# A hybrid four-branch trunk on one Trainium2 core: branch outputs through the weight ring, keys and values of the window branch in its own stage, z gates among the first SSD convolutions

## The chip, the cores and the metric

The kernel runs on one core of one Trainium2 chip. The metric is the device time of one execution in microseconds (us). The engines are called PE (TensorE, the matmuls), DVE (VectorE), ACT (ScalarE), POOL (GpSimd) and SP (SyncE, which here only issues DMAs). Each has its own queue and executes it in order; engines wait for each other through semaphores.

## The reference

One layer, a sequence of 512 tokens, model width 2048, everything in float32. A single combined projection of the normalized input feeds four token mixers of width 1024 and four merge gates:

```python
h = rms_norm(x, norm_w[l])
proj = jnp.einsum("bsd,dn->bsn", h, w_in[l])
(aq, ak, av, ag, bq, bk, bv, bg, cxbc, cdt, cz, dglu, dg, mg) = jnp.split(proj, _split_points(), axis=-1)
ya = diff_attention(aq, ak, av, lam, lam_init, subln_w, bias_a) * silu(ag)   # A: 8 heads, causal
yb = sliding_window_attention(bq, bk, bv, sinks, bias_b) * silu(bg)          # B: window 128, 16 q / 4 kv heads
yc = ssd_mixer(cxbc, cdt, cz, ...)                                           # C: Mamba-2 SSD, gated by silu(cz)
yd = conformer_conv(dglu, ...) * silu(dg)                                    # D: GLU, conv of 31 taps, LayerNorm
up = jnp.einsum("bsir,ird->bsid", branches, w_branch[l])
merged = jnp.sum(jax.nn.sigmoid(mg) * up, axis=2)
x = rms_norm(x + jnp.einsum("bsd,de->bse", merged, w_out[l]), final_norm_w)
```

(The calls are shortened.) `ssd_mixer` first runs a convolution of 4 taps and a SiLU over its x, B and C channels, then works in chunks of 128 tokens with decay matrices from `dt`.

## The kernel before

**Precision.** Each float32 matmul is done as three products of split operands: `x = hi + lo` with both halves in the fast fp32 format, and `hi*hi + lo*hi + hi*lo` summed in PSUM. So each weight piece goes three steps: a DMA into a `wr` tile, an ACT cast to `wh`, a DVE subtraction to `wl` (L289, L296, L297). The hidden state's halves are `hh` and `hl`.

**The weight ring.** `wr`, `wh` and `wl` have three buffers each in pool `wp`. `build_sequence` writes down the order of all weight pieces of the program; `next_piece` hands out the next one and makes pieces up to PLA = 6 ahead, but not beyond `state["limit"]`. SP issues all of these loads.

**Projections.** `proj(c)` is 128 output columns over all 512 tokens: 16 steps of the contraction by three products, 48 products of 512 columns (L410 to L412), into one of three PSUM banks `acc`. The result is multiplied by `rb` (the token norm) on DVE. `silu_of` is two DVE steps around an ACT sigmoid (L604 to L606).

**Stages in time.**
- 0 to about 785 us: the merge gates and one value projection, in groups; their results go to DRAM (`gate_d`).
- to about 1060: SSD (branch C). For each of two groups: convolutions `conv4` of B, C and four x tiles (L693 to L700, four taps on DVE at L697), for the first group the dt chain, then chunk by chunk the decay matrices `se` (L761 to L772 on DVE, ACT and POOL) and their matmuls (L778, L781), then the z gates and the output.
- to about 1440: the conformer convolution (31 taps on DVE, L835), then its LayerNorm and activation to about 1482.
- to about 1711: differential attention (branch A), head by head: queries and keys (L933 to L948), scores (L952, L953), softmax, transposes (L1005), outputs (L1009).
- to about 1873: window attention (branch B) with the same kinds of steps (scores at L952 too, L1069 to L1100).
- to about 2200: the merge. For each branch, `load_y` brings its output back from `y_d` as `yraw` and splits it (L1115, L166, L167) into `yh` and `yl`; four blocks of columns follow, each with four w_branch pieces of 24 products (L482 to L484), a multiplication by the gate tile `gt` and a sum. The pools `yq` of `yh` and `yl` take the space in which `hh` and `hl` lay.
- then the output projection and the final norm, to 2424.

Branch outputs go to `y_d`; some SiLU gates and branch B's keys and values, projected right behind SSD, go to DRAM (`silu_d`, `kv_d`) and come back later. POOL issues those DMAs.

**Order.** The program is written stage by stage, but a scheduler (`TCKW = {"schedule_with_timeline_sim": True}`) sets each engine's order, so work of neighbouring stages is mixed. The weight sequence and the pools bound what it can move.

Of the kernel before, what the change touches and what calls it, by code (L numbers as in the profile page):

```python
# [11 lines left out]
F32 = mybir.dt.float32  # L12
F32R = mybir.dt.float32r
AF = mybir.ActivationFunctionType
ALU = mybir.AluOpType
# [36 lines left out]
def build_sequence():  # L52
    seq = []

    def proj(col):
        for half in range(2):
            seq.append(("p", col, half))

    for half in range(2):
        for col in (CB, CC):  # L60
            seq.append(("p", col, half))
    for r in range(2):
        for kp in range(KH // 2):
            seq.append(("s0", r, kp))
    for col in EARLY[2:]:
        proj(col)
    for gi in range(NGROUP):
        for k in range(KH):
            seq.append(("s1", gi, k))
        for r in rest(gi):  # L70
            for kp in range(KH // 2):
                seq.append(("s2", gi, r, kp))
    for g in range(2):
        for j in range(4):
            if CX + (g * 4 + j) * P not in EARLY:
                proj(CX + (g * 4 + j) * P)
        for j in range(4):
            proj(CZ + (g * 4 + j) * P)
    for j in range(2):
        proj(BK + j * P)  # L80
        proj(BV + j * P)
    for c in range(NB):
        proj(DV + c * P)
        proj(DGT + c * P)
        proj(DG + c * P)
        proj(AG + c * P)
    for j in range(4):
        proj(BG + j * P)
    for h in range(8):
        proj(AQ + h * P)  # L90
        proj(AK + h * P)
    for j in range(8):
        proj(BQ + j * P)
        if j >= 4:
            proj(BG + j * P)
    for br in BRANCHES:
        for nb in range(4):
            for k2 in range(NB // 2):
                seq.append(("u", br, nb, k2))
    for eb in range(3):  # L100
        for k2 in range(KT // 2):
            seq.append(("o", eb * S, k2 * 2, 2, S))
    for eh in range(2):
        for k4 in range(KT // 4):
            seq.append(("o", 3 * S + eh * 256, k4 * 4, 4, 256))
    return seq
# [3 lines left out]
def hybrid_trunk(ctx, tc, x, norm_w, w_in, diff_lambda, diff_subln_w, swa_sinks, ssd_conv_w,  # L110
# [88 lines left out]
    pieces = {}  # L199
    first_s = next(i for i, key in enumerate(seq) if key[0] == "s1")  # L200
    first_late = len(seq) - KT // 4
    state = {"made": 0, "used": 0, "limit": first_s}
# [222 lines left out]
    raw_d = dram.tile([len(EARLY), P, S], F32, name="raw_d")  # L425
    kv_d = dram.tile([4, P, S], F32, name="kv_d")
    silu_d = dram.tile([3, NB, P, S], F32, name="silu_d")
# [10 lines left out]
    mge = open_pool("mge", 3, "right")  # L438
    state["limit"] = first_late
    sums = {}  # L440
# [262 lines left out]
    dtw = load_dt()  # L703
    for g in range(2):
        bT, cT = hold(), hold()
        conv4(CB + g * P, 8 + g, bT)
        conv4(CC + g * P, 10 + g, cT)
        xT = []
        for j in range(4):
            xj = keep("yh")  # L710
            conv4(CX + (g * 4 + j) * P, g * 4 + j, xj)
            xT.append(xj)
# [24 lines left out]
        for t in range(NT - 1):  # L737
# [10 lines left out]
            prev[t + 1] = pv  # L748
        sz = []
        for j in range(4):  # L750
            z = keep("yl")
            silu_of(proj(CZ + (g * 4 + j) * P), z)
            sz.append(z)
        for t in range(NT):
# [51 lines left out]


    for j in range(2):
        for i, c0 in enumerate((BK, BV)):
            kv = hold()  # L810
            V.tensor_tensor(kv, proj(c0 + j * P), rb, op=ALU.mult)
            G.dma_start(kv_d[2 * j + i], kv)
    vtoks = []
# [15 lines left out]
    def conv_taps(c, pad, y):  # L829
# [10 lines left out]
        return [lambda j=j: tap(j) for j in range(31)]  # L840

    def stored_silu(i, c, w):
        sg = hold()
        silu_of(proj(w + c * P), sg)
        G.dma_start(silu_d[i, c], sg)

# [39 lines left out]
    A.copy(rbs, rd)  # L886
    for j in range(4):
        stored_silu(2, j, BG)
# [140 lines left out]
    for j in range(2):  # L1029
        kk, kl = [yp.tile([P, S], F32R, tag="yh", name="kk") for _ in range(2)], [hold(F32R), hold(F32R)]  # L1030
        k = early()
        G.dma_start(k, kv_d[2 * j])
        keys(k, kk, kl)
        kd += [(kk[m], kl[m]) for m in range(2)]
        vT = early()
        G.dma_start(vT, kv_d[2 * j + 1])
        pt = tr_tile()
# [68 lines left out]
    gp = open_pool("gp", 2, "right")  # L1106
    rp = open_pool("rp", 2, "right")
    up = open_pool("up", 4, "right")
    sets = [[acc_tile, acc_tile, acc_tile, lambda: s_tile(0)], [lambda: s_tile(1), tr_tile, tr_tile, o_tile]]

    def load_y(bi):
        his, los = [], []
        for q in range(2):
            raw = rp.tile([P, 4, S], F32, tag="raw", name="yraw")
            G.dma_start(raw, y_d[BRANCHES[bi], 4 * q:4 * q + 4].rearrange("k p s -> p k s"))  # L1115
            hi = yq[bi % 2].tile([P, 4, S], F32R, tag="y", name="yh")
            lo = yq[2 + bi % 2].tile([P, 4, S], F32R, tag="y", name="yl")
            split(raw, hi, lo)
            his.append(hi)
            los.append(lo)  # L1120
        return his, los
# [13 lines left out]

    ys = load_y(0)
    for bi, br in enumerate(BRANCHES):
        for nb in range(4):
# [23 lines left out]
        if bi < 3:  # L1162
            ys = ys_next
    close_pool("up", "rp", "gp", "mp")
    lastp = open_pool("lastp", 4)
# [119 lines left out]
```

## Time and profile before

| | |
|---|---|
| median of 3 runs | 2423.55 us (2423.54 to 2424.19) |
| profiled execution | 2425.63 us, span 2423.9 us |
| mean granted clock of PE | 0.990 |
| PE, DVE, ACT, POOL busy | 98%, 66%, 38%, 15% of the span |

The span runs from the first to the last instruction of the profiled execution; the rest of its own time lies around it. "Busy" counts an engine's instructions, not its waits. The granted clock is the share of full speed that PE was given; its levels are 1.2 and 2.4 GHz, so 0.5 is the lower one throughout a stretch. A window's row gives for each engine the busy time in that stretch.

### The profile page before, as it was taken

The numbers are of one execution on the slowest core, as the hardware profiler recorded it, in microseconds if no ns is written. First come the engines' busy times: TensorE is split into PE (matmuls) and PEld (weight loads), VectorE is DVE, ScalarE is ACT, GpSimd is POOL, SyncE is SP. The second block draws the span as 40 slices with busy tenths as digits, with TensorE's granted clock in tenths as the row PEclk, the third lists the DMA queues.
The fourth block names the chain that finished last, engine by engine and source line by source line (L and its number), as shares of the span: only waits on it lengthen the run. The fifth ranks groups of instructions, "written<-read, shape, count | busy, mean of one in ns | idle before, by whom it ended". The sixth has DMA issues, their size and how long they took to land.

```text
span 2423.9 us, 29417 instructions
## 1 busy us (share of the span) xinstructions
PE 2367.8 (98%) x11141; PEld 1949.8 (80%) x11141; DVE 1597.2 (66%) x2550; ACT 931.6 (38%) x1434; POOL 368.4 (15%) x428
## 2 busy tenths in 40 slices
PE   8989999999999999999999999999998999999998
PEld 7868888888887877888888888888776788888888
DVE  6697877777776678558887887766666444334323
ACT  5344444444544344222222235555465222122222
POOL 1000000000001023110101034222101012233101
PEclk9999999999999999999999999999899999999999
DMA  8554555555556444344343355333232744443423
GB/s 255 148 165 153 171 174 156 163 165 165 165 167 185 115 124 117 108 140 111 106 118 105 109 153 174 102 99 105 74 92 87 257 166 147 148 148 119 150 98 111
DMA packets 299115, 340.22 MB, mean 140 GB/s; under 512 B 14862, under 2 KB 203659, under 8 KB 298974
## 3 DMA queue, kind: packets, MB, share of 16 engines
q1 hardware_dynamic: 267742, 247.84, 34.7%
q0 software_dynamic: 27744, 84.21, 10.3%
q10 hardware_dynamic: 3488, 6.30, 0.8%
q8 instruction: 87, 1.43, 0.2%
q14 instruction: 54, 0.44, 0.1%
HBM read 296.79 MB, written 41.51 MB: 140 GB/s over the span
## 4 chain that ended last, share of the span: by engine, by line
PE 64%; issue 3%; DVE 3%; DMA 1%; ACT 0%; POOL 0%; POOLq 0%; DVEq 0%; ACTq 0%
PE acc L411 11%; PE acc L412 11%; PE acc L410 11%; PE acc L482 2%; PE acc L483 2%; PE acc L484 2%; PE s L482 1%; PE tr L483 1%; PE tr L482 1%; PE s L483 1%; PE tr L484 1%; PE s L484 1%; PE acc L1183 1%; PE acc L1184 1%; PE acc L1185 1%
## 5 line engine op out<-in xcount | busy, mean ns | idle before, releaser
L296 ACT CAST wh<-wr 128x1024 fp32r<-128x1024 f32 x268 | 281.9, 1052 | 782.8 <-PE acc L411 310.6
L297 DVE TENSOR_TENSOR wl<-wr,wh 128x1024 fp32r<-128x1024 f32 x268 | 339.2, 1266 | 337.3 <-ACT wh L296 335.3
L410 PE MATMUL acc<-hh,wh 128*128 128x512 f32 x1312 | 515.4, 393 | 0.0
L412 PE MATMUL acc<-hh,wl 128*128 128x512 f32 x1312 | 515.1, 393 | 0.0
L411 PE MATMUL acc<-hl,wh 128*128 128x512 f32 x1312 | 514.7, 392 | 0.0
L411 PEld LDWEIGHTS acc<-hl,wh 128*128 128x128 f32 x1312 | 246.9, 188 | 51.3 <-issue 2.5
L410 PEld LDWEIGHTS acc<-hh,wh 128*128 128x128 f32 x1312 | 246.9, 188 | 51.2 <-issue 2.0
L412 PEld LDWEIGHTS acc<-hh,wl 128*128 128x128 f32 x1312 | 246.9, 188 | 50.5 <-issue 1.5
L218 ACT CAST wh<-wr 128x1024 fp32r<-128x1024 f32 (+1 forms) x152 | 155.4, 1029 | 192.8 <-PE o L484 76.3
L219 DVE TENSOR_TENSOR wl<-wr,wh 128x1024 fp32r<-128x1024 f32 (+1 forms) x152 | 180.2, 1192 | 38.9 <-ACT wh L218 38.7
L835 DVE SCALAR_TENSOR_TENSOR keep_yl<-pad,cols,keep_yl 128x512 f32<-128x512 f32 x240 | 179.9, 750 | 5.6
L497 POOL DMA_DIRECT2D gate_d<-e x64 | 34.7, 542 | 600.8 <-ACT e L496 599.6
L1159 POOL TENSOR_TENSOR m<-m,u 128x512 f32<-128x512 f32 x48 | 73.5, 1562 | 185.7 <-DVE u L1158 185.7
L222 ACT CAST wh<-t 128x512 fp32r<-128x512 f32 x72 | 44.7, 620 | 111.0 <-PE tr L484 77.0
L482 PE MATMUL acc<-wh,yh 128*128 128x512 f32 x192 | 75.6, 394 | 9.7 <-ACT yh L166 9.7
L581 PE MATMUL acc<-wl,hh 128*128 128x512 f32 x200 | 78.5, 393 | 1.4 <-DVE wl L219 1.3
L582 PE MATMUL acc<-wh,hl 128*128 128x512 f32 x200 | 77.2, 391 | 0.3 <-DVE hl L446 0.3
L483 PE MATMUL acc<-wl,yh 128*128 128x512 f32 x192 | 75.5, 393 | 0.0
L580 PE MATMUL acc<-wh,hh 128*128 128x512 f32 x200 | 75.3, 391 | 0.2 <-DVE e L570 0.2
L484 PE MATMUL acc<-wh,yl 128*128 128x512 f32 x192 | 74.5, 390 | 0.0
L269 DVE TENSOR_TENSOR t<-wr,t 128x1024 f32<-128x1024 f32 x32 | 39.2, 1224 | 52.0 <-DMA wr<-in_w_in_dram 52.0
L242 DVE TENSOR_TENSOR vr<-vr,wr 128x512 f32<-128x512 f32 x72 | 49.5, 687 | 33.5 <-DMA wr<-in_w_in_dram 33.5
(484 smaller groups left out, 4968.8 us busy)
## 6 DMA issues: line engine op xcount, KB each, us to landing
wr<-in_w_in_dram SPq DMA_DIRECT2D x328, 512.0 KB, 3.9
wr<-in_w_branch_dram SPq DMA_DIRECT2D x64, 512.0 KB, 3.7
vr<-in_w_in_dram SPq DMA_DIRECT2D x36, 512.0 KB, 4.3
gate_d<-e POOLq DMA_DIRECT2D x64, 256.0 KB, 3.0
gt<-gate_d POOLq DMA_DIRECT2D x16, 1024.0 KB, 5.5
wr<-in_w_out_dram SPq DMA_DIRECT2D x32, 512.0 KB, 3.8
yraw<-y_d POOLq DMA_DIRECT2D x8, 1024.0 KB, 6.4
y_d<-t POOLq DMA_DIRECT2D x24, 256.0 KB, 3.1
```

Of the source, the lines that this page charges most:

```text
L218: A.copy(hi, srcs[0])
L219: V.tensor_tensor(lo, srcs[0], hi.bitcast(F32), op=ALU.subtract)
L296: A.copy(hi, raw)
L297: V.tensor_tensor(lo, raw, hi.bitcast(F32), op=ALU.subtract)
L410: T.matmul(acc, lhsT=wh[:, k, :], rhs=xh, start=(n == 0), stop=False)
L411: T.matmul(acc, lhsT=wh[:, k, :], rhs=xl, start=False, stop=False)
L412: T.matmul(acc, lhsT=wl[:, k, :], rhs=xh, start=False, stop=(n == last))
L482: T.matmul(acc, lhsT=x[0], rhs=w[0], start=first, stop=False)
L483: T.matmul(acc, lhsT=x[0], rhs=w[1], start=False, stop=False)
L484: T.matmul(acc, lhsT=x[1], rhs=w[0], start=False, stop=last)
L581: T.matmul(bank[t], lhsT=x[0], rhs=wl[:, j], start=False, stop=False, skip_group_check=True)
L835: V.scalar_tensor_tensor(y, pad[:, j:j + S], w, y, op0=ALU.mult, op1=ALU.add)
```

## The change

It has three parts.

1. `load_y` no longer has tiles of its own (`rp`, 1 MB each, issued by POOL). It takes four `wr` tiles of 512 KB from the weight ring, loaded by SP. The weight pieces of the merge may not be made before the first `load_y` (`limit = first_up`).
2. The four projections of keys and values of branch B (BK, BV) stand behind branch A's queries and keys in the sequence and feed branch B directly; `kv_d` is gone. Two of four stored BG gates take their place behind SSD, two stay at the LayerNorm.
3. The four z gates of group 0 stand between the first convolutions (`gate_z`), ahead of the dt chain; in the sequence of weights CX 2 to 7 follow them, and the z gates of group 1 follow those.

```diff
-    for g in range(2):
-        for j in range(4):
-            if CX + (g * 4 + j) * P not in EARLY:
-                proj(CX + (g * 4 + j) * P)
-        for j in range(4):
-            proj(CZ + (g * 4 + j) * P)
+    for j in range(4):
+        proj(CZ + j * P)
+    for j in range(2, 8):
+        proj(CX + j * P)
+    for j in range(4, 8):
+        proj(CZ + j * P)
     for j in range(2):
-        proj(BK + j * P)
-        proj(BV + j * P)
+        proj(BG + j * P)
...
-    for j in range(4):
+    for j in range(2, 4):
         proj(BG + j * P)
     for h in range(8):
         proj(AQ + h * P)
         proj(AK + h * P)
+    for j in range(2):
+        proj(BK + j * P)
+        proj(BV + j * P)
...
-    state["limit"] = first_late
+    state["limit"] = first_up
...
+        if g == 0:
+            gate_z()
         conv4(CB + g * P, 8 + g, bT)
+        if g == 0:
+            gate_z()
         conv4(CC + g * P, 10 + g, cT)
-        xT = []
         for j in range(4):
+            if g == 0 and j < 2:
+                gate_z()
             xj = keep("yh")
...
     for j in range(2):
-        for i, c0 in enumerate((BK, BV)):
-            kv = hold()
-            V.tensor_tensor(kv, proj(c0 + j * P), rb, op=ALU.mult)
-            G.dma_start(kv_d[2 * j + i], kv)
+        stored_silu(2, j, BG)
...
-        G.dma_start(k, kv_d[2 * j])
+        V.tensor_tensor(k, proj(BK + j * P), rb, op=ALU.mult)
...
-        G.dma_start(vT, kv_d[2 * j + 1])
+        V.tensor_tensor(vT, proj(BV + j * P), rb, op=ALU.mult)
...
-        for q in range(2):
-            raw = rp.tile([P, 4, S], F32, tag="raw", name="yraw")
-            G.dma_start(raw, y_d[BRANCHES[bi], 4 * q:4 * q + 4].rearrange("k p s -> p k s"))
-            hi = yq[bi % 2].tile([P, 4, S], F32R, tag="y", name="yh")
-            lo = yq[2 + bi % 2].tile([P, 4, S], F32R, tag="y", name="yl")
-            split(raw, hi, lo)
-            his.append(hi)
-            los.append(lo)
+        his = [yq[bi % 2].tile([P, 4, S], F32R, tag="y", name="yh") for _ in range(2)]
+        los = [yq[2 + bi % 2].tile([P, 4, S], F32R, tag="y", name="yl") for _ in range(2)]
+        for kp in range(NB // 2):
+            raw = wp.tile([P, 2, S], F32, tag="wr", name="wr")
+            nc.sync.dma_start(raw, y_d[BRANCHES[bi], 2 * kp:2 * kp + 2].rearrange("k p s -> p k s"))
+            r = kp % 2 * 2
+            split(raw, his[kp // 2][:, r:r + 2], los[kp // 2][:, r:r + 2])
...
     ys = load_y(0)
+    state["limit"] = first_late
```

How the change moves instructions is shown at three places. An order row has the line, the operation, the tiles and the shape, and a count where it repeats. Line numbers of the changed kernel are some higher: projections L413 to L415, the z gates L606 to L608, scores L961 and L962.

**SSD, DVE, in the midst of the first group's decay matrices** (`se`). Before, the steps of convolutions (L693 to L700, on `ev`) stand between them:

```order
L761 TENSOR_SCALAR se<-se,acum 128x128 x8
L695 TENSOR_SCALAR ev<-ev,cols 128x512
L297 TENSOR_TENSOR wl<-wr,wh 128x1024
L697 SCALAR_TENSOR_TENSOR ev<-ev,cols 128x512
L769 TENSOR_TENSOR se<-se,t 128x1024
L697 SCALAR_TENSOR_TENSOR ev<-ev,cols 128x512
L785 SCALAR_TENSOR_TENSOR keep_yh<-keep_yh,dcol,o 128x128 x4
```

Now the same decay steps have a weight's `wl` and the steps of a z gate (L606, L608) between them:

```order
L780 TENSOR_TENSOR t<-tr,tri 128x128
L608 TENSOR_TENSOR keep_yl<-keep_yl,ev 128x512
L762 TENSOR_TENSOR prev_b<-prev_b,s_6677 128x512
L797 SCALAR_TENSOR_TENSOR keep_yh<-keep_yh,dcol,o 128x128 x4
L773 TENSOR_SCALAR se<-se,acum 128x128 x8
L300 TENSOR_TENSOR wl<-wr,wh 128x1024
L781 TENSOR_TENSOR se<-se,t 128x1024
L606 TENSOR_TENSOR keep_yl<-acc,rb 128x512
```

The convolutions of the second group have moved ahead, beside the dt chain; group 1's z gates stand where they stood.

**The end of differential attention, PE.** The last head's transposes (`tr`) and outputs (`o`) before, followed by the first scores of window attention (`s<-kk,qs`) and only then by a projection product (L410):

```order
L1021 MATMUL tr<-ident,t 128x128 x4
L1005 MATMUL tr<-ident,pr 128x128
L1009 MATMUL o<-keep_yh,aT 128x128
L1005 MATMUL tr<-ident,pr 128x128 x5
L1009 MATMUL o<-keep_yh,aT 128x128 x5
L1005 MATMUL tr<-ident,pr 128x128 x4
L1009 MATMUL o<-keep_yh,aT 128x128 x4
```

The same transposes now, one step of them, with projection products ahead and behind:

```order
L413 MATMUL acc<-hh,wh 128x512
L1018 MATMUL o<-keep_yh,aT 128x128
L1014 MATMUL tr<-ident,pr 128x128 x5
L414 MATMUL acc<-hl,wh 128x512
L415 MATMUL acc<-hh,wl 128x512
```

Twenty products of a key or value projection stand there up to the next output step, and pieces as long stand at the steps behind it.

**The end of window attention, SP and PE.** SP's loads before, all that is left of the program's projection weights and then the merge's and the output's (`y_d` came back on POOL, behind POOL's last three stores into it):

```order
L289 DMA wr<-in_w_in_dram 128x8x128 x158
L289 DMA wr<-in_w_branch_dram 128x2x512 x64
L289 DMA wr<-in_w_out_dram 128x2x512 x24
L289 DMA wr<-in_w_out_dram 128x4x256 x8
L1236 DMA out_dram<-keep_yh 128x512 x4
```

And now, with four branch-output loads ahead of the first branch weight and behind the tenth, the 26th and the 42nd:

```order
L292 DMA wr<-in_w_in_dram 128x8x128 x158
L1124 DMA wr<-y_d 128x2x512 x4
L292 DMA wr<-in_w_branch_dram 128x2x512 x10
L1124 DMA wr<-y_d 128x2x512 x4
L292 DMA wr<-in_w_branch_dram 128x2x512 x16
L1124 DMA wr<-y_d 128x2x512 x4
```

On PE, the last transposes and outputs of the window stage before, and the first products with a branch output (L482, `yh`):

```order
L1094 MATMUL o<-pT,keep_yh 64x128 x4
L1087 MATMUL tr<-ident,pb 128x128 x4
L1094 MATMUL o<-pT,keep_yh 64x128 x8
L482 MATMUL acc<-wh,yh 128x512
L483 MATMUL acc<-wl,yh 128x512
L482 MATMUL acc<-wh,yh 128x512
```

And now, where the last scores (L961, L962) stand on both sides of the first branch products (L484):

```order
L961 MATMUL s_14753<-kk,qs 128x256
L962 MATMUL s_14753<-hd,qs 128x256
L961 MATMUL s_14778<-kk,qs 128x256
L962 MATMUL s_14778<-hd,qs 128x256
L484 MATMUL acc<-wh,yh 128x512 x3
L961 MATMUL s_14782<-kk,qs 128x256
L962 MATMUL s_14782<-hd,qs 128x256
L485 MATMUL acc<-wl,yh 128x512
```

The first branch products have moved ahead of the window stage's last scores; 94 of the first block's 96 products stand ahead of its last outputs.

## Rows read from the trace of the kernel before

**Rows 1.** The page's first part: busy us (share of span) x instructions

```profile
PE 2367.8 (98%) x11141; PEld 1949.8 (80%) x11141; DVE 1597.2 (66%) x2550; ACT 931.6 (38%) x1434; POOL 368.4 (15%) x428
```

**Rows 2.** Windows, full stretch: length, busy us per engine, PEclk, DMA share, GB/s

```profile
1200.00:1300.00 100.00, 100.00 (x443) 82.84 (x442) 84.17 (x108) 23.55 (x26) 9.14 (x11) 1.00 0.39 111
```

**Rows 3.** Windows, SSD stage: length, PE PEld DVE ACT POOL busy, PEclk

```profile
820.00:880.00 60.00, 58.60 (x270) 47.36 (x269) 42.75 (x93) 24.67 (x29) 7.31 (x9) 1.00 0.35 98
...
880.00:910.00 30.00, 28.60 (x181) 22.64 (x180) 28.31 (x54) 10.92 (x11) 7.76 (x10) 1.00 0.43 132
910.00:940.00 30.00, 24.31 (x130) 19.15 (x129) 29.00 (x47) 19.15 (x22) 12.06 (x10) 0.99 0.25 73
940.00:960.00 20.00, 20.00 (x96) 17.05 (x96) 13.91 (x20) 4.83 (x7) 7.93 (x11) 0.92 0.71 207
```

**Rows 4.** Windows, tails of differential (1692 on) and window attention (1852 on)

```profile
1692.00:1698.00 6.00, 3.59 (x20) 2.66 (x19) 4.87 (x18) 4.37 (x17) 1.05 (x1) 0.95 0.32 87
1698.00:1711.00 13.00, 8.11 (x33) 6.47 (x31) 5.01 (x13) 4.75 (x17) 3.57 (x6) 0.50 0.25 61
1711.00:1715.00 4.00, 3.86 (x11) 3.02 (x12) 3.46 (x8) 1.24 (x2) 3.37 (x3) 0.57 0.00 0
1852.30:1857.00 4.70, 2.02 (x13) 1.39 (x12) 4.12 (x17) 2.98 (x7) 0.55 (x1) 1.00 0.46 167
1857.00:1865.00 8.00, 6.71 (x38) 5.31 (x38) 5.07 (x35) 5.67 (x20) 0.00 (x0) 0.57 0.01 3
1865.00:1873.00 8.00, 5.83 (x59) 3.74 (x54) 5.00 (x25) 5.43 (x19) 0.55 (x1) 1.00 0.09 33
1873.00:1882.00 9.00, 0.00 (x0) 0.00 (x0) 0.26 (x1) 1.75 (x1) 5.70 (x9) 0.60 0.76 261
1882.00:1886.00 4.00, 3.80 (x11) 3.05 (x12) 3.43 (x2) 2.04 (x2) 0.76 (x1) 0.61 1.03 391
```

**Rows 5.** Waits of PE: line and releaser: total us, times, longest

```profile
PE acc L482 <- ACT yh L166: 9.7, 1, 9.7
...
PE s L952 <- DVE qs L937: 2.4, 1, 2.4
```

**Rows 6.** Timeline of POOL, ACT and DVE around 1873 to 1895

```profile
1874.09 1.54 POOL L1115 DMA_DIRECT2D yraw<-y_d  x2
...
1880.25 1.90 ACT L166 CAST yh<-yraw 128x2048 fp32r<-128x2048 f32 x1 [8.46 <-DMA yraw<-y_d]
...
1889.33 1.05 ACT L296 CAST wh<-wr 128x1024 fp32r<-128x1024 f32 x1 [4.50 <-PE s L484]
...
1890.42 1.23 DVE L297 TENSOR_TENSOR wl<-wr,wh 128x1024 fp32r<-128x1024 f32 x1 [3.26 <-ACT wh L296]
```

**Rows 7.** Lines on DVE, 880 to 940: busy us, mean ns | idle before

```profile
L697 DVE SCALAR_TENSOR_TENSOR ev<-ev,cols 128x512 f32<-128x512 f32 x15 | 17.5, 1166 | 0.2
```

**Rows 8.** Timeline of DVE and POOL, 905 to 945: start, us, engine, line

```profile
906.21 1.66 DVE L761 TENSOR_SCALAR se<-se,acum 128x128 f32<-128x128 f32 x8
...
911.48 2.85 DVE L697 SCALAR_TENSOR_TENSOR ev<-ev,cols 128x512 f32<-128x512 f32 x1
...
921.21 0.75 DVE L697 SCALAR_TENSOR_TENSOR ev<-ev,cols 128x512 f32<-128x512 f32 x1
...
926.02 4.73 DVE L761 TENSOR_SCALAR se<-se,acum 128x128 f32<-128x128 f32 x8
...
911.33 2.45 POOL L772 TENSOR_TENSOR se<-se,hd 128x1024 f32<-128x1024 f32 x1 [6.52 <-ACT se L771]
```

**Rows 9.** Timeline of ACT at the LayerNorm and the first queries

```profile
1439.94 0.59 ACT L886 COPY rbs<-tr 128x512 f32<-128x512 f32 x1 [1.08 <-PE tr L190]
...
1484.35 2.54 ACT L936 CAST qs<-ev 64x512 fp32r<-64x512 f32 x4
```

**Rows 10.** DMA issues: KB each, median us to landing; whole span, then 1870:2000

```profile
wr<-in_w_branch_dram SPq DMA_DIRECT2D x64, 512.0 KB, 3.7
...
wr<-in_w_branch_dram SPq DMA_DIRECT2D x20, 512.0 KB, 6.0
```

More of the change, by code (lines that the diff above doesn't have):

```diff
@@ L200, in hybrid_trunk @@
     first_s = next(i for i, key in enumerate(seq) if key[0] == "s1")
+    first_up = next(i for i, key in enumerate(seq) if key[0] == "u")
     first_late = len(seq) - KT // 4
@@ L425, in hybrid_trunk @@
     raw_d = dram.tile([len(EARLY), P, S], F32, name="raw_d")
-    kv_d = dram.tile([4, P, S], F32, name="kv_d")
     silu_d = dram.tile([3, NB, P, S], F32, name="silu_d")
@@ L704, in hybrid_trunk, with gate_z @@
     for g in range(2):
+        sz = []
+        def gate_z():
+            z = keep("yl")
+            silu_of(proj(CZ + (g * 4 + len(sz)) * P), z)
+            sz.append(z)
         bT, cT = hold(), hold()
+        xT = []
+        if g == 0:
+            gate_z()
         conv4(CB + g * P, 8 + g, bT)
+        if g == 0:
+            gate_z()
         conv4(CC + g * P, 10 + g, cT)
-        xT = []
         for j in range(4):
+            if g == 0 and j < 2:
+                gate_z()
             xj = keep("yh")
@@ L748, in hybrid_trunk @@
             prev[t + 1] = pv
[L749 to L753, printed above, removed]
+        while len(sz) < 4:
+            gate_z()
         for t in range(NT):
@@ L805, in hybrid_trunk, with stored_silu @@
             G.dma_start(y_d[2, g * 4 + j], y)
+    def stored_silu(i, c, w):
+        sg = hold()
+        silu_of(proj(w + c * P), sg)
+        G.dma_start(silu_d[i, c], sg)
     for j in range(2):
-        for i, c0 in enumerate((BK, BV)):
-            kv = hold()
-            V.tensor_tensor(kv, proj(c0 + j * P), rb, op=ALU.mult)
-            G.dma_start(kv_d[2 * j + i], kv)
+        stored_silu(2, j, BG)
     vtoks = []
@@ L840, in conv_taps @@
         return [lambda j=j: tap(j) for j in range(31)]
[L842 to L845, printed above, removed]
     for c in range(NB):
@@ L886, in hybrid_trunk @@
     A.copy(rbs, rd)
-    for j in range(4):
+    for j in range(2, 4):
         stored_silu(2, j, BG)
@@ L1106, in hybrid_trunk @@
     gp = open_pool("gp", 2, "right")
-    rp = open_pool("rp", 2, "right")
     up = open_pool("up", 4, "right")
@@ L1111, in load_y @@
     def load_y(bi):
-        his, los = [], []
-        for q in range(2):
-            raw = rp.tile([P, 4, S], F32, tag="raw", name="yraw")
-            G.dma_start(raw, y_d[BRANCHES[bi], 4 * q:4 * q + 4].rearrange("k p s -> p k s"))
-            hi = yq[bi % 2].tile([P, 4, S], F32R, tag="y", name="yh")
-            lo = yq[2 + bi % 2].tile([P, 4, S], F32R, tag="y", name="yl")
-            split(raw, hi, lo)
-            his.append(hi)
-            los.append(lo)
+        his = [yq[bi % 2].tile([P, 4, S], F32R, tag="y", name="yh") for _ in range(2)]
[5 more added lines that the diff above has]
+            split(raw, his[kp // 2][:, r:r + 2], los[kp // 2][:, r:r + 2])
         return his, los
@@ L1163, in hybrid_trunk @@
             ys = ys_next
-    close_pool("up", "rp", "gp", "mp")
+    close_pool("up", "gp", "mp")
     lastp = open_pool("lastp", 4)
```

## The prediction

> **What bounds the kernel now.** I read the engines' shares first: TensorE (PE) is busy 98% of the span and VectorE (DVE) 66% [rows 1]. So PE's work sets the time, and a change that leaves the matmuls as they are can win only PE's idle time and the stretches in which PE runs at the lower of its two clock levels. I looked for these with a table of windows, each as its length less PE busy, plus PE busy times (1 less granted clock). A full stretch gives the price of a product: 443 PE instructions in 100 us [rows 2], 0.226 us each; a projection of 48 products is 10.8 us.
>
> Three places that the change touches are not full.
> - The SSD stage: 1.40 us idle in 820 to 880, 1.40 in 880 to 910, 5.69 in 910 to 940; then 20 us at 0.92 cost 1.6 and the 0.99 before it 0.2. That is **10.3 us** [rows 3]. DVE is the reason from 880 on: busy 28.3 and 29.0 of 30 us.
> - The tail of differential attention: idle 2.41, 4.89 and 0.14; clock 0.95, 0.50 and 0.57 on 3.59, 8.11 and 3.86 us of work cost 0.2, 4.1 and 1.7. That is **13.4 us** [rows 4]. The longest wait is for the next stage's queries, 2.4 us [rows 5].
> - The tail of window attention: idle 2.68, 1.29, 2.17, 9.00 and 0.20; the clocks of 0.57 and 0.61 cost 2.9 and 1.5. That is **19.7 us** [rows 4]. 9.7 us of it is the longest wait of PE in the whole trace, for the first cast of a branch output [rows 5]. That load is issued by POOL at 1874.09, the cast starts at 1880.25 and the products after it [rows 6].
>
> Together 43.4 us is all that can be won here; the rest of PE's idle time lies at the start, in the gate stage and in the output tail, which the change leaves alone.
>
> **The change part by part.**
>
> *z gates among the first SSD convolutions.* Nothing is added or removed: four z projections go to before the dt chain, and four convolutions that ran beside group 0's decay matrices go with their taps to 825 to 880. In 880 to 940 DVE spent 17.5 us on 15 taps, 1.17 us each [rows 7], where a tap alone takes 0.75 and one beside POOL's multiply 2.85 [rows 8]. The order shows z multiplies in their place. A z gate has two DVE steps, taken at a tap's 0.75, so four gates are 6 us against 17.5 of taps: DVE falls from 57.3 of 60 us to about 46. What left has to fit into 820 to 880, where DVE has 17.3 us free. Over 820 to 940 DVE stays at 100.1 of 120 us, 83%; the 100 us of rows 2 ran full at 84%. So I take the gain near the whole: **+8** of 10.3 (waits of the decay chain itself stay), bounds 0 and 10.3. If the early stretch has no room, the dt chain is late next and the gain is 0.
>
> The row of 2.85 us against 0.75 stands on POOL's multiply beside it. The Trainium skill, "SBUF — State Buffer", § "SBUF: two separate sides", says a DVE operation with two SBUF inputs fully blocks against a GpSimd operation that reads SBUF. The trace agrees for the tap; but eight scale steps with one tensor input also took 4.73 us together [rows 8], which the rule as worded doesn't cover. By the rule a z multiply can be caught as a tap was, four at (2.85 - 0.75) or 8.4 us, and the stage's gain would be near nothing (2406.5 in all). By the rows, taps lost 0.42 on average, and four lose 1.7.
>
> *Keys and values of branch B in their own stage.* Four projections (43 us of PE) leave the place behind SSD, where two BG projections and the conformer's first take over, and land in the tail of differential attention. The order shows pieces of about 20 products (4.6 us) between the last head's steps, where before nothing stood. The waits there are 2.4 us and less [rows 5], so each is covered, and with PE fed the clock should hold. Four stores and four loads on POOL go; POOL's queue was nearly idle and no PE wait names them, so 0. DVE's four multiplies by rb are the same work. What stays is the queries' own chain and the first piece after it: **+12** of 13.4, bounds 9 and 13.4.
>
> The price is cover at the layer norm. Two of the four BG projections are gone from there, and some query projections take part of their place: by the order 179 products stand between the last statistics product and the first scores, 40.4 us; before it was 219, 49.4 us. From the norm's row of scales to the first query cast 44.4 us pass [rows 9], and with the projections part of DVE's and ACT's work in that chain goes too. The stall is 0 to 6; I take **-2**.
>
> *Branch outputs through the weight ring.* Two 1 MB loads on POOL become four of 512 KB on SP, ahead of the first branch weights. They are not behind POOL's last store, and the raw data can land during the window stage. The casts still go where the hidden state's halves lay, so they start after the last projection product. What follows it then: that product's three short steps, 0.75 each (the nearest row); y0's ACT cast 1.05 and DVE difference 1.23 [rows 6], with window steps between some 0.9; y1's difference 1.23, which frees a slot of the ring of three; the first branch weight 3.7 [rows 10]; its cast 1.05. The sum is 11.4, less what overlaps of the first cast about 1.4: the first u product some 10 us after, its low half 12. PE has 2 us of window work by then [rows 4]; the stall is 8 to 10, and about 2 us go to the lower clock behind it. So 10 to 12 of the 19.7 remain; the other window steps are covered, since 94 u products of 0.226 now stand ahead of the last of them. **+8**, bounds 4 (the later weights at the 6.0 us landings of the crowded stretch [rows 10], and their window chain exposed) and 14 (y raw and cast before the last projection's end). Weights of the merge are no longer fetched in the window stage, as three were before; this is in the sum.
>
> Three later loads pass through the same ring. From a free weight slot to the need are two pieces of 24 products, 10.8 us; in it lie four y differences 4.9, the weight's load 3.7 and its casts 2.3: 10.9. With landings of 6.0 it is 13.2. So 0 to 2.4 for each; I take **-1** in all (0 to -7).
>
> Sum: 8 + 12 - 2 + 8 - 1 = **25**. The profiled execution took 2425.6 (span 2423.9), so 2400.6 for one like it; the median of the runs is 2.1 below it: **2398.5**.
>
> **The rivals** (against 2423.55).
> - *SSD stays bound by DVE*: the taps fill 820 to 880 and the dt chain waits. For it: DVE is the full engine wherever convolutions meet decay steps [rows 3], and taps grow beside POOL [rows 8]. Against: 83% over both halves. SSD gives 1: 2405.5.
> - *The ring keeps the wait*: the first product is paced by the transfer, not by who issues it. Then only POOL's issue of 1.5 us is won at the window tail, 6.5 less than in the sum: 2405. The page that speaks for it is the Trainium skill's "DMA: Bandwidth & Descriptors", § "Issuing engines are not separate DMA queues": another issuing engine saves only the time of issuing. Against: here the load's place in the queue moves too, ahead of the window's last store.
> - *The norm's cover is gone*: the stall is its bound of 6 and PE loses 2 more at the lower clock behind it, as at 1711 [rows 4]: 8 us rather than 2, 2404.5.
> - *Slower*: the later y loads hold the weights. Their casts stand ahead of the weights' on ACT and DVE, and their target is free only when the block before has ended; if each of the three makes PE wait over 8.3 us (a chain of 19.1 in place of 10.9), the 25 are gone. At 10 each it takes 2429. Against: the merge has no PE wait now, with weights spaced by 24 products.
> - *No change*: the in-order PE queue meets the same waits at other rows, the tails' idle only moves: 2423.5.
>
> **How the numbers follow.** The forecast 0.55; SSD 0.13; the ring 0.14, of which 0.06 by the page's rule; the norm 0.08; slower 0.05; no change 0.05. A change below 0.2%, 4.8 us, can't be told from none here. The first four are faster: 0.90; same 0.05; slower 0.05. The best case (10.3 + 13.4 + 14) ends at 2386, the low end 2384. Two of the three middle rivals at once end near 2412, the high end; what is left out above are the last two and three at once.
>
> **What would show it.** PE's idle time in the SSD stage below 3 us and DVE there below 85%; no PE wait over 1 us between the last head's steps and clock 1.0 there; the wait for the first cast (L168 or a w_branch piece) 8 to 10 us instead of 9.7, with the window's last steps after it and no second gap; a new wait of 0 to 6 us before the first scores of differential attention; none over 2.4 us at the second to fourth y loads. Wrong would be: a wait for y or its weights over 15 us in the merge, or a dt chain that holds PE.

## The result, and the profile after

| | before | changed |
|---|---|---|
| median | 2423.55 us | 2395.2 us (4 runs, 2391.45 to 2397.34) |
| ratio | 1 | 0.9881, 95% interval 0.9864 to 0.9898 |
| profiled execution, span | 2425.63, 2423.9 | 2394.65, 2392.9 |
| mean granted clock of PE | 0.990 | 0.996 |

The forecast was 2398.5. The changed kernel is 28 us faster by the medians and 31.0 by the two profiled spans. The page's first part of the changed kernel, which answers to [rows 1]:

```profile
PE 2357.9 (99%) x11141; PEld 1942.3 (81%) x11141; DVE 1601.8 (67%) x2558; ACT 930.8 (39%) x1440; POOL 356.9 (15%) x412
```

PE has the same 11141 instructions, so the gain can only be idle time and clock. Windows of the changed kernel at the places of [rows 3] and [rows 4] (columns as in [rows 2]; later stages lie some us earlier in time there and are found by their tiles. The first two SSD rows hold other work than before, since the first decay step, L773, starts at 912.47 instead of 868.25):

```profile
820.00:880.00 60.00, 60.00 (x267) 49.41 (x266) 40.27 (x62) 16.52 (x20) 2.87 (x11) 1.00 0.39 106
880.00:910.00 30.00, 30.00 (x142) 24.87 (x141) 22.01 (x47) 12.05 (x16) 1.97 (x6) 1.00 0.34 91
910.00:940.00 30.00, 29.86 (x166) 23.17 (x166) 28.82 (x56) 13.85 (x15) 7.34 (x5) 1.00 0.42 122
940.00:960.00 20.00, 20.00 (x137) 15.88 (x133) 14.34 (x35) 9.25 (x10) 6.63 (x5) 1.00 0.43 123
...
1440.00:1484.00 44.00, 41.28 (x191) 34.51 (x192) 30.73 (x70) 21.55 (x43) 9.37 (x10) 0.96 0.41 119
...
1660.00:1700.00 40.00, 40.00 (x202) 33.79 (x201) 23.61 (x44) 15.82 (x33) 8.72 (x10) 1.00 0.40 105
1826.00:1834.00 8.00, 6.39 (x46) 4.83 (x44) 5.25 (x19) 4.67 (x9) 0.55 (x1) 1.00 0.03 9
1834.00:1840.00 6.00, 2.84 (x12) 1.74 (x12) 5.37 (x15) 4.70 (x9) 0.00 (x0) 0.70 0.78 249
1840.00:1850.00 10.00, 8.78 (x30) 7.07 (x31) 7.31 (x29) 6.47 (x18) 0.00 (x0) 0.67 0.70 228
...
1880.00:2200.00 320.00, 320.00 (x1437) 265.20 (x1436) 135.90 (x142) 79.12 (x82) 77.52 (x58) 1.00 0.49 168
```

The SSD stage is full (0.14 us idle), the tail of differential attention is full at full clock (1660 to 1700), a new gap of 3.4 us stands before the first scores (2.7 of it in 1440 to 1484), the window tail has 6.0 us of gaps and 3 to 4 at the lower clock, and the merge has no idle time at all.

PE's waits of the changed kernel, against [rows 5]:

```profile
PE s L353 <- DMA xt<-in_x_dram: 5.2, 1, 5.2
PE tr L582 <- DVE e L570: 3.9, 1, 3.9
PE acc L413 <- DVE ev L942: 3.4, 1, 3.4
PE s L961 <- DVE mx L1078: 3.3, 2, 1.7
PE acc L484 <- ACT wh L299: 2.6, 1, 2.6
```

The wait of 9.7 us for the first cast of a branch output is gone. In its place stand three smaller ones at the window tail: two for a softmax step (`mx`, 3.3 together) and 2.6 for the first branch weight. The third row is the new wait at the LayerNorm. The first two rows lie in the start and the gate stage.

The same reading for every kernel of this study, idle time of PE plus what the lower clock cost, in us, each summed over windows of 10 us (window length less PE busy, plus busy times 1 less clock):

| kernel | gates, start | SSD | norm | diff. tail | window tail | merge | output tail |
|---|---|---|---|---|---|---|---|
| before | 19.9 | 10.2 | 0 | 13.5 | 20.6 | 0 | 7.9 |
| changed | 19.3 | 0.1 | 4.6 | 0 | 9.8 | 0 | 8.1 |
| e1, branch outputs back | 20.3 | 0.4 | 3.4 | 0 | 23.6 | 0 | 7.9 |
| e2, keys and values back | 20.2 | 0.1 | 0 | 15.9 | 9.2 | 0 | 8.5 |
| e3, z gates back | 17.7 | 9.6 | 4.7 | 0 | 10.7 | 0 | 8.1 |
| e4, BG gates at the norm | 24.9 | 0.4 | 0 | 0 | 8.3 | 0 | 8.6 |
| e5, weights first | 24.8 | 0.3 | 4.5 | 0 | 0.7 | 3.9 | 8.1 |
| e6, POOL issues, ring tiles | 20.4 | 0.6 | 4.5 | 0 | 9.8 | 0 | 8.0 |
| e7, SP issues, own tiles | 21.3 | 0.3 | 5.6 | 0 | 23.1 | 0 | 7.8 |
| e8, both mends | 21.7 | 0.5 | 0 | 0 | 0.4 | 0 | 8.6 |
| e9, before with decay on DVE | 25.0 | 1.8 | 0 | 11.4 | 21.8 | 0 | 7.8 |

The changed kernel gains 10.1 + 13.5 + 10.8 and loses 4.6: 29.8 of the 31.0 us between the spans. The rest is in the gate stage and the rounding of the clock. That stage, which no edit touches, varies between 17.7 and 25.0 from one profiled execution to another, about the width of the 6 us over which single runs of the changed kernel spread.

### The profile page after: what moved, and what is told of

Read it like the earlier page. It is cut to its first block, busy times and chain, and to the rows that moved or that the text cites. A ratio compares the mean times of both kernels' runs of the same rounds, so it can differ in the third digit from the quotient of the medians.

```text
span 2392.9 us, 29464 instructions
## 1 busy us (share of the span) xinstructions
PE 2357.9 (99%) x11141; PEld 1942.3 (81%) x11141; DVE 1601.8 (67%) x2558; ACT 930.8 (39%) x1440; POOL 356.9 (15%) x412
## 4 chain that ended last, share of the span: by engine, by line
PE 91%; issue 6%; DVE 1%; DMA 1%; POOL 0%; ACT 0%; POOLq 0%; DVEq 0%; ACTq 0%
PE acc L415 13%; PE acc L413 13%; PE acc L414 13%; PE acc L484 4%; PE acc L485 4%; PE acc L486 4%; PE s L484 2%; PE tr L486 2%; PE tr L485 2%; PE s L485 2%; PE s L486 2%; PE tr L484 2%; PE acc L583 2%; PE acc L584 2%; PE acc L582 2%
## 5 line engine op out<-in xcount | busy, mean ns | idle before, releaser
L413 PE MATMUL acc<-hh,wh 128*128 128x512 f32 x1312 | 514.8, 392 | 3.4 <-DVE ev L942 3.4
L415 PE MATMUL acc<-hh,wl 128*128 128x512 f32 x1312 | 515.5, 393 | 0.0
L413 PEld LDWEIGHTS acc<-hh,wh 128*128 128x128 f32 x1312 | 246.9, 188 | 55.2 <-ACT qs L945 3.8
L415 PEld LDWEIGHTS acc<-hh,wl 128*128 128x128 f32 x1312 | 246.7, 188 | 51.0 <-issue 2.4
L484 PE MATMUL acc<-wh,yh 128*128 128x512 f32 x192 | 74.6, 396 | 2.6 <-ACT wh L299 2.6
```

Source lines behind the costliest of these rows:

```text
L413: T.matmul(acc, lhsT=wh[:, k, :], rhs=xh, start=(n == 0), stop=False)
L415: T.matmul(acc, lhsT=wl[:, k, :], rhs=xh, start=False, stop=(n == last))
L484: T.matmul(acc, lhsT=x[0], rhs=w[0], start=first, stop=False)
```

## The experiments

Each ran beside the kernel before, whose median was 2426.2 us for e1 to e4, 2426.8 for e5 to e8 and 2425.1 for e9, some 2 to 3 us above the first 2423.55. So ratios are compared, and "in the first scale" means the ratio times 2423.55; the changed kernel's 0.9881 is 2394.7 there.

### e1: branch outputs loaded as before

```diff
-            raw = wp.tile([P, 2, S], F32, tag="wr", name="wr")
-            nc.sync.dma_start(raw, y_d[BRANCHES[bi], 2 * kp:2 * kp + 2].rearrange("k p s -> p k s"))
+            raw = rp.tile([P, 4, S], F32, tag="raw", name="yraw")
+            G.dma_start(raw, y_d[BRANCHES[bi], 4 * q:4 * q + 4].rearrange("k p s -> p k s"))
...
-    state["limit"] = first_up
+    state["limit"] = first_late
```

> The changed kernel with part 1 undone: branch outputs loaded as 1 MB tiles by POOL, w_branch weights prefetched in the window stage. Theory (the load's place and room make the wait): the window tail loses again 19 to 20 us, of which 9.7 are one wait for the first cast of a branch output; total 2395 + 10 = 2405, range 2402 to 2408. Rival (only POOL's issue time was saved): 1.5 us more, 2396.5.

Measured 0.9930 (0.9917 to 0.9942), 2406.6 in the first scale: 11.9 us above the changed kernel. The table shows the place, 23.6 at the window tail. PE's wait, and POOL's timeline (start, us, engine, line):

```profile
PE acc L484 <- ACT yh L168: 9.9, 1, 9.9
```

```profile
1854.13 0.54 POOL L1109 DMA_DIRECT2D y_d<-t  x1 [5.50 <-DVE t L1108]
1854.66 1.53 POOL L1124 DMA_DIRECT2D yraw<-y_d  x2
```

The load is again issued right behind the last store of a window output, and the wait of [rows 5] is back. The window tail loses more than the 19 to 20 us expected, and the total is 2 us above the 10 expected, within its range.

### e2: keys and values of branch B behind SSD

```diff
-        stored_silu(2, j, BG)
+        for i, c0 in enumerate((BK, BV)):
+            kv = hold()
+            V.tensor_tensor(kv, proj(c0 + j * P), rb, op=ALU.mult)
+            G.dma_start(kv_d[2 * j + i], kv)
...
-    for j in range(2, 4):
+    for j in range(4):
         stored_silu(2, j, BG)
```

> The changed kernel with part 2 undone: keys and values of branch B projected behind SSD and kept in DRAM, all four BG gates at the LayerNorm. Theory: the tail of differential attention loses its 13.4 us again and the LayerNorm its 5 us no more, so 2395 + 13.4 - 5 = 2403.5, range 2400 to 2407; no PE wait for a query's accumulator before the first scores. Rival (the tail was filled by another part of the change, or the waits only moved): within 2 us of the changed kernel's 2395.

Measured 0.9924 (0.9911 to 0.9936), 2405.1: 10.4 above the changed kernel (8.4 expected). Windows of its norm and its tail of differential attention, and the wait for the next stage's queries:

```profile
1440.00:1490.00 50.00, 50.00 (x225) 41.41 (x225) 38.62 (x60) 26.88 (x41) 22.03 (x25) 1.00 0.66 195
1682.00:1692.00 10.00, 6.25 (x24) 4.15 (x22) 7.27 (x22) 4.20 (x19) 3.78 (x6) 0.70 0.38 95
1692.00:1702.00 10.00, 5.05 (x19) 4.10 (x20) 2.68 (x7) 3.79 (x15) 1.12 (x2) 0.50 0.14 37
```

```profile
PE s L963 <- DVE qs L948: 2.4, 1, 2.4
```

The tail is like that of [rows 4], with the same 2.4 us for the queries; it loses 15.9 us where the kernel before lost 13.5. The norm is full. Both signs of this part lie where the theory has them.

### e3: z gates behind their group's convolutions

```diff
-    for j in range(4):
-        proj(CZ + j * P)
-    for j in range(2, 8):
-        proj(CX + j * P)
-    for j in range(4, 8):
-        proj(CZ + j * P)
+    for g in range(2):
+        for j in range(4):
+            if CX + (g * 4 + j) * P not in EARLY:
+                proj(CX + (g * 4 + j) * P)
+        for j in range(4):
+            proj(CZ + (g * 4 + j) * P)
...
-        if g == 0:
-            gate_z()
```

> The changed kernel with part 3 undone: z gates behind the convolutions of their group as before. Theory (DVE was the bound beside the decay matrices): PE loses 9 to 10.5 us in the SSD stage, DVE there at 94% or more between 880 and 940; total 2395 + 10 = 2405, range 2402 to 2407. Rival (BG and the conformer's first projections behind SSD are what filled it): 0 to 3 us more, 2395 to 2398.

Measured 0.9918 (0.9904 to 0.9931), 2403.7: 9.0 above the changed kernel. The stage's windows:

```profile
880.00:910.00 30.00, 27.98 (x176) 21.84 (x175) 28.41 (x57) 12.24 (x13) 6.61 (x8) 1.00 0.41 123
910.00:940.00 30.00, 25.02 (x135) 20.47 (x135) 28.89 (x46) 17.27 (x20) 11.25 (x10) 0.97 0.31 88
```

DVE is busy 95% and 96% and PE has its gaps again, though BG and the conformer's projections stand behind SSD here as in the changed kernel. The rival that these filled the stage falls.

### e4: all four BG gates at the LayerNorm

```diff
-    for j in range(2):
-        proj(BG + j * P)
...
-    for j in range(2, 4):
+    for j in range(4):
         proj(BG + j * P)
```

> The changed kernel with all four stored BG gates at the LayerNorm, none behind SSD. Theory (the new wait at the norm is missing cover of two projections): the wait of 3.4 us for DVE's step L942 and the lower clock behind it go, 5 us, and SSD stays full because the conformer's projections move up: 2390, range 2388 to 2393. Rival (SSD's second group needs the two BG gates): it loses 3 to 6 us there and the total stays at 2393 to 2397.

Measured 0.9852 (0.9839 to 0.9866), 2387.7: 7.0 below the changed kernel. SSD and the norm:

```profile
880.00:960.00 80.00, 79.57 (x416) 63.79 (x415) 65.81 (x137) 34.60 (x37) 15.36 (x15) 1.00 0.41 113
...
1400.00:1490.00 90.00, 90.00 (x424) 75.07 (x423) 68.36 (x131) 48.65 (x89) 32.00 (x33) 1.00 0.50 145
```

The norm is full with two more projections there, and SSD does not need them: 0.4 us idle. So the loss at the norm was missing cover, and the price was avoidable. The stage table explains 5.8 of the 7.0 (4.6 at the norm, 1.5 at the window tail, less 0.3 in SSD); the rest is within the intervals.

### e5: three weights ahead of the first branch output

```diff
-    state["limit"] = first_up
+    state["limit"] = first_up + 3
```

> The changed kernel with the first three w_branch pieces allowed ahead of the first branch output in the weight ring. Theory (what is left of the window tail is the first weight's load and casts behind two branch-output pieces): the wait for the first weight, 2.6 us, and the scores' waits behind it go, PE's loss at the window tail falls from 9.7 to 3 to 5 us; total 2395 - 5.5 = 2389.5, range 2387 to 2392. Rival (the loss is set by the window's own softmax steps on DVE, which carry the casts too): the same loss at other rows, 2394 to 2397.

Measured 0.9853 (0.9838 to 0.9868), 2387.9: 6.8 below the changed kernel. The first product with a branch output, on PE's timeline:

```profile
1833.63 0.50 PE L484 MATMUL acc<-wh,yh 128*128 128x512 f32 x1 [0.24 <-ACT yh L168]
```

It waits 0.24 us and the window tail loses 0.7 in place of 9.8 (3 to 5 were expected). The rival (softmax steps set the loss) falls: these steps are unchanged, and the products now stand ahead of them as cover. In the profiled execution 3.9 us came back 70 us later:

```profile
1903.98 1.65 PE L484 MATMUL acc<-wh,yh 128*128 128x512 f32 x3 [2.70 <-ACT wh L299]
```

This is the weight behind the second branch's outputs, which the prediction had priced at 0 to 2.4 for each load. In the changed kernel's and e8's trace no such wait stands.

### e6 and e7: who issues, and into which tiles

e6 keeps the ring's tiles and lets POOL issue; e7 lets SP issue into two 1 MB tiles of a pool of their own, with the weights prefetched as before.

```diff
# e6
-            nc.sync.dma_start(raw, y_d[BRANCHES[bi], 2 * kp:2 * kp + 2].rearrange("k p s -> p k s"))
+            G.dma_start(raw, y_d[BRANCHES[bi], 2 * kp:2 * kp + 2].rearrange("k p s -> p k s"))
# e7
-            raw = wp.tile([P, 2, S], F32, tag="wr", name="wr")
+            raw = rp.tile([P, 4, S], F32, tag="raw", name="yraw")
+            nc.sync.dma_start(raw, y_d[BRANCHES[bi], 4 * q:4 * q + 4].rearrange("k p s -> p k s"))
```

> The changed kernel with its branch-output loads issued by POOL, in the same ring tiles of 512 KB; in POOL's order the first three stand ahead of the window's last five stores. Theory (place in the order and room count, not the engine): window tail within 2 us of the changed kernel's, total 2394 to 2398. Rival (SP instead of POOL is what gained): the wait of nearly 10 us for the first branch output returns, 2403 to 2406.

> The changed kernel with branch outputs loaded by SP, but as 1 MB tiles of a pool of their own, opened when the window stage's pools close, and w_branch weights prefetched as before. Theory (room is the cause: those tiles lie where the window stage's tiles lay, so the load can't start before its end): the 9 us gap stays, total 2403 to 2406. Rival (POOL's queue, behind the last store, was the cause): most of the 10 us stays won, 2394 to 2398.

Measured: e6 0.9878 (0.9865 to 0.9892), 2394.0, the same as the changed kernel; e7 0.9927 (0.9914 to 0.9939), 2405.9, nearly e1. The first branch-output load and the window's last store on POOL in e6:

```profile
1794.41 0.74 POOL L1124 DMA_DIRECT2D wr<-y_d  x1 [13.58 <-DVE wl L300]
...
1875.22 0.55 POOL L1109 DMA_DIRECT2D y_d<-t  x1 [14.76 <-DVE t L1108]
```

And SP's first load in e7, with PE's longest wait:

```profile
1857.56 18.74 SPq L1124 DMA_DIRECT2D yraw<-y_d  x4
```

```profile
PE acc L484 <- ACT yh L168: 8.8, 1, 8.8
```

SP's own wait for that load:

```profile
SPq L1124 <- DVE t L1108: 24.0, 1, 24.0
```

In e6 POOL issues the load 81 us before the last store: a ring slot is free, so the scheduler could place it early. In e7 SP issued its last weight ahead of the load by 1833.3 and then the load only at 1857.56, as the window stage ends (its last store starts at 1857.78). POOL's queue can't hold it there. The data are not the reason either: the first branch loaded is C, which e6 could read at 1794.41. The wait of 24.0 us names the window stage's last output step, L1108, on a tile `t` of that stage, and the space of the load's tiles belongs to the window stage's pools until then. So room decides, not the engine.

### e8: both mends

```diff
-    state["limit"] = first_up
+    state["limit"] = first_up + 3
...
-    for j in range(2, 4):
+    for j in range(4):
         proj(BG + j * P)
```

(With e4's other lines.)

> The changed kernel with both edits: all four BG gates at the LayerNorm, and three w_branch pieces ahead of the first branch output. Theory: both gains add, 5 at the norm and 5.5 at the window tail, 2384.5, range 2382 to 2388. Rival (either gives its gain back elsewhere): 2389 or more.

Measured 0.9821 (0.9808 to 0.9835), 2380.2 in the first scale (median 2382.68 beside 2426.8). The gains add: 14.5 us below the changed kernel. Of the 43.4 us that the prediction counted as the most to be won, nothing over 0.5 is left in any of the four stages. The window tail:

```profile
1830.00:1850.00 20.00, 19.56 (x118) 15.82 (x117) 15.85 (x59) 15.36 (x34) 0.55 (x1) 1.00 0.45 145
```

### e9: the decay multiplies of the kernel before on DVE

```diff
-                G.tensor_tensor(row, row, cT[:, t * P:(t + 1) * P].unsqueeze(1).to_broadcast([P, 8, P]),
+                V.tensor_tensor(row, row, cT[:, t * P:(t + 1) * P].unsqueeze(1).to_broadcast([P, 8, P]),
                                 op=ALU.mult)
...
-                G.tensor_tensor(sqs, sqs, sq, op=ALU.add)
+                V.tensor_tensor(sqs, sqs, sq, op=ALU.add)
```

> The kernel before with two of POOL's tensor operations of the SSD stage put on DVE: the multiply of the decay row by C (L772) and the sum of squares (L795). It disputes what makes DVE full between 880 and 940. Theory (DVE's taps, scale steps and products are stretched while POOL reads tensors: 17.5 us of taps in place of 11.2, 9.8 of scale steps in place of 6.6, 6.6 of products in place of 4.9): these means return to 0.75, 0.21 and 1.23, which gives DVE 11 us back for 7 of added work; PE's loss in the stage falls from 10.3 to 5 to 8.5 us, total 2 to 5 us less. Rival (the stretch comes from something else, the casts on ACT or the DMAs): the means stay, DVE gets 7 us of work more, and the stage loses 14 to 17 us, total 4 to 7 us more.

Measured 0.9965 (0.9954 to 0.9977), 8.5 us less than the kernel before in the first scale, without any of the change; 2 to 5 were expected. DVE's lines from 880 to 940 (busy us, mean ns | idle), against [rows 7], and the windows against [rows 3]:

```profile
L697 DVE SCALAR_TENSOR_TENSOR ev<-ev,cols 128x512 f32<-128x512 f32 x18 | 13.4, 745 | 0.2
...
L761 DVE TENSOR_SCALAR se<-se,acum 128x128 f32<-128x128 f32 x32 | 6.8, 278 | 0.7 <-DMA se<-acum_d 0.7
```

```profile
880.00:910.00 30.00, 29.76 (x182) 23.39 (x183) 29.00 (x59) 13.34 (x13) 4.61 (x11) 1.00 0.48 136
910.00:940.00 30.00, 30.00 (x160) 24.84 (x159) 28.17 (x56) 18.69 (x20) 2.62 (x4) 1.00 0.40 111
```

The tap is at 745 ns again, where it was 1166, and PE is nearly full although DVE is as busy as before: it now does more steps in the same time. The stage's loss falls to 1.8, where 5 to 8.5 were expected. So POOL's operations did stretch DVE's steps. How much of the 8.4 us in the table comes from that is not separated: PE's wait of 1.6 us for POOL's own sum (L795) went with the sum, and the scheduler put 81 projection products in place of 55 between the last decay products and the product that reads it.

## Why the prediction was right

The five terms, by the table of stages:

| term | forecast | measured |
|---|---|---|
| SSD | +8 (0 to 10.3) | +10.1 |
| differential tail | +12 (9 to 13.4) | +13.5 |
| norm | -2 (0 to -6) | -4.6 |
| window tail | +8 (4 to 14) | +10.8 |
| merge | -1 (0 to -7) | 0 |
| sum | 25 | 29.8 |

The four terms that moved have their sign, and each lies within its bounds; the differential tail's 13.5 is its bound of 13.4 within the rounding. The three gains were taken 2.1, 1.5 and 2.8 us too small and the merge's loss 1 too large; the norm's loss, 2.6 too small, goes the other way. That leaves 4.8 between the sums, and the median is 3.3 below the forecast. That it came so near is in part luck: 7.4 us of misses one way stand against 2.6 the other.

**SSD.** The result is as argued, and e3 shows that this part alone gives it. The measure that I leaned on, DVE's share of busy time, says less than I thought. From 820 to 940 DVE is busy 40.3, 22.0 and 28.8 us in 60, 30 and 30, 76% in place of 83%, but part of the decay steps now lies behind 940. The windows from the first to the last decay step of group 0, before and changed:

```profile
868.00:931.00 63.00, 57.58 (x331) 45.04 (x329) 59.64 (x115) 30.55 (x34) 21.62 (x20) 1.00 0.34 102
```

```profile
912.00:970.00 58.00, 57.86 (x332) 45.67 (x331) 51.16 (x103) 28.30 (x31) 20.03 (x13) 1.00 0.40 116
```

DVE falls from 95% to 88% there and is still at 96% between 910 and 940, against "below 85%" in the list of what would show it; and e9 has PE nearly full with DVE at 95%. What changed is how soon DVE takes up a step that PE needs. Before, PE's two longest waits in this stage were for POOL:

```profile
PE tr L190 <- POOL rs L185: 2.3, 1, 2.3
PE tr L798 <- POOL t L795: 1.6, 1, 1.6
```

Both POOL steps stand behind DVE's: the sum (L795) behind the multiplications by the z gate (L789, now L801), which DVE began 6.1 us after PE's last decay product of the group (it ended at 915.80) and begins 1.1 us after it in the changed kernel (it ends at 958.89). The rows before and changed:

```profile
921.87 2.50 DVE L789 TENSOR_TENSOR keep_yh<-keep_yh,keep_yl 128x512 f32<-128x512 f32 x4
```

```profile
959.97 1.29 DVE L801 TENSOR_TENSOR keep_yh<-keep_yh,keep_yl 128x512 f32<-128x512 f32 x2
```

With about as many projection products between (55 and 52), PE no longer waits for the sum. The rival that the taps fill the early stretch did not come about.

e9 shows that POOL's tensor operations stretched DVE's steps. The Trainium skill, "SBUF — State Buffer", § "SBUF: two separate sides", says that a DVE operation in a two-port performance mode, or one with two SBUF inputs against a GpSimd operation that reads SBUF, blocks against GpSimd. For the taps the runs agree (1166 ns beside POOL, 745 without). The scale step L761, with one tensor input and a scalar column, was stretched too: 374 ns before, 278 in e9. My text said that the rule doesn't cover it; that section names `tensor_scalar` among the operations that can run in a two-port mode, so it may, and no run here tells the mode. By the rule I had z gates stretched as the taps were and no gain. That did not come: the z gates' DVE steps beside the first group's decay matrices met no multiply or sum on POOL and took 0.68 to 0.69 us each. This was the scheduler's doing, and so does not speak against the rule; one that ran beside POOL's multiplications in the kernel before (at 877.73) took 1.38.

**Differential tail.** Covered by pieces of about 20 products, as worked out; without them, in e2, this tail loses 15.9 us.

**Norm.** This is the term that was mis-sized: -2 taken, 4.6 lost, 3.4 of it idle and 1.2 at the lower clock, for which the term had nothing. The count of products was right (179 against 219), but it was set against the wrong chain. The rows of the changed kernel:

```profile
1407.91 0.59 ACT L895 COPY rbs<-tr 128x512 f32<-128x512 f32 x1 [3.01 <-PE tr L192]
...
1418.34 0.67 DVE L942 SCALAR_TENSOR_TENSOR ev<-acc,rb 64x512 f32<-64x512 f32 x1
...
1440.27 0.61 ACT L945 CAST qs<-ev 64x512 fp32r<-64x512 f32 x1
...
1441.88 0.69 DVE L942 SCALAR_TENSOR_TENSOR ev<-acc,rb 64x512 f32<-64x512 f32 x1
...
1442.72 0.47 PE L413 MATMUL acc<-hh,wh 128*128 128x512 f32 x1 [3.41 <-DVE ev L942]
```

From the norm's row of scales to the first query cast are 32.4 us, 12.0 less than before, while the cover fell by 9.0: this chain would not have held PE. PE stood still earlier, ahead of the 132nd of the 179 products, because that one needs an accumulator, of which there are three, and DVE had not emptied it. Each query projection is emptied in two steps (L942); the first ran at 1418.34 and the second only at 1441.88, in DVE's queue behind a weight's `wl` and the norm's last multiplications. e4 gives the cover back and the loss is gone.

**Window tail.** The chain was right in its order and its length. The rows of the changed kernel, PE, DVE, SP and ACT (start, us, engine, line):

```profile
1830.22 0.40 PE L415 MATMUL acc<-hh,wl 128*128 128x512 f32 x1
...
1832.34 1.22 DVE L169 TENSOR_TENSOR yl<-wr,yh 128x1024 fp32r<-128x1024 f32 x1
...
1834.16 2.36 DVE L169 TENSOR_TENSOR yl<-wr,yh 128x1024 fp32r<-128x1024 f32 x2
...
1835.40 34.46 SPq L292 DMA_DIRECT2D wr<-in_w_branch_dram  x9
...
1840.13 1.04 ACT L299 CAST wh<-wr 128x1024 fp32r<-128x1024 f32 x1 [1.39 <-DMA wr<-in_w_branch_dram]
...
1841.22 1.65 PE L484 MATMUL acc<-wh,yh 128*128 128x512 f32 x3 [2.63 <-ACT wh L299]
```

From the end of the last projection product, 1830.62, to the first u product are 10.6 us; the forecast was 10. Inside it the first weight took 4.7 us from its issue to its cast, not 3.7. PE had more window work meanwhile than the 2 us taken: it stood still for 6.0 us in three pieces instead of 8 to 10 in one, and the lower clock cost 3.8 instead of 2. So the tail keeps 9.8 of 20.6 us, where 10 to 12 of 19.7 were forecast; 0.9 of the 2.8 us by which this gain was taken too small lies in the two counts of the kernel before. The first weight is issued by SP at 1835.40, when the second `yl` has released a slot of the ring. So the gain came from where the loads may be placed, and what was left of the wait came from the ring of three, the latter as forecast. e6 and e7 split it: the ring's tiles with POOL as issuer keep the gain, SP with late tiles loses it. The Trainium skill, "DMA: Bandwidth & Descriptors", § "Issuing engines are not separate DMA queues", says that another issuing engine saves only the time of issuing; e6 agrees (0.9878 against 0.9881). The forecast of the rival that leant on it, a gain of 1.5 us in all at this place, fell, because the change also moved the load to earlier tiles. My text put the gain on the place in POOL's queue behind the last store; e7 shows that the room for the tiles, free only when the window stage ends, is by itself enough to hold the load there.

**Merge.** No wait in the changed kernel, and one of 2.7 us in e5, against 0 to 2.4 for each. The slower rival did not occur.

## What to carry to other kernels

Where PE is 98% busy, sum its idle time and its half-clock time by stage, and ask of each edit which stage's sum it touches: the sums predicted the total within a few us, and each undo gave back its own stage. Count cover up to the first product that needs a bank still to be emptied, not only up to the step that ends the chain, and ask how long a step waits in its engine's queue rather than how busy the engine is. A prefetch can only start when its target tile is free: look at which pool's tiles the load's space comes from before changing the queue that issues it. When loads share a short ring with what is needed first, order the ring by need: three weights ahead of the branch outputs were worth 6.8 us, and moving cover to the place that had lost it 7.0.

## What the runs showed of the hardware

POOL's tensor operations slow DVE steps more widely than expected: a step with one tensor input was stretched too (L761, 374 to 278 ns when POOL's operations were taken away), and 8 steps beside POOL's sums took 4.73 us against 1.66 [rows 8]. Taking two POOL operations onto DVE, which was 95% busy there, made that stage faster by 8 us. The clock fell behind some gaps: the window tail's 6.0 us of idle time in the changed kernel cost 3.8 more at a granted clock of 0.70 and 0.67, and in e8 without the gap the clock was 1.00 there. It did not fall behind all: behind 3.4 us of idle time at the norm it was 0.83 in the changed kernel and 1.00 in e1 (both from 1443 to 1453). That the gate stage differs by up to 7 us between executions, with the same instructions, was not settled.
